# Block 2 of a two-block kernel: own buffers for the meta chunk's matrix, decay gates between the first projections, inverses' copies and second solve in a given order

## The chip, the cores and the metric

The kernel runs on one core of one Trainium2 chip. The metric is the device time of one launch in microseconds. A core has five engines that take their instructions in order, each from its own queue, and that wait for one another with semaphores: TensorE (PE, matrix products), VectorE (DVE), ScalarE (ACT, activations and copies), GpSimd (POOL) and SyncE (SP), which here issues the DMAs. All DMAs of this program that matter below are issued from SP's queue.

## The reference, cut to what matters

Two blocks follow each other. The first (an RWKV-like block) and the mixture of experts at the end are untouched. The change lies in the mixer of the second block: a gated delta rule in two directions, beside a Fourier branch.

```python
proj = hn @ w_in                       # f_in, qkv, z, ab, gate_f, gate_d
f_mix = jnp.real(jnp.fft.fft2(fg, axes=(1, 3), norm="ortho"))
y_f = f_mix.reshape(bsz, seq_len, F_WIDTH) @ w_fourier
qkv = jax.nn.silu(depthwise_conv_centred(qkv, conv_w))
q, k, v = jnp.split(qkv, [QK_WIDTH, 2 * QK_WIDTH], axis=-1)   # then l2-normalised q, k
g_f = -jnp.exp(a_log_f) * jax.nn.softplus(a_f + dt_bias_f)    # decay, and the same backward
beta_f = jax.nn.sigmoid(b_f)
...
# gated_delta_chunked, chunks of 64, 8 heads, both directions
g = jnp.cumsum(g, axis=-1)
decay = jnp.where(lower, jnp.exp(g[..., :, None] - g[..., None, :]), 0.0)
a_mat = jnp.where(strict, (k_beta @ k.T) * decay, 0.0)
t_mat = triangular_solve(eye + a_mat, eye)      # inverse of a 64x64 triangle per chunk and head
u = t_mat @ (v * beta); w = t_mat @ (k_beta * exp(g))
# scan over chunks: v_new = u - w S;  o = q S + qk v_new;  S = S dec + k^T v_new
...
merged = sigmoid(gate_f) * y_f + sigmoid(gate_d) * y_d
return merged @ w_out
```

Sixteen meta tokens stand ahead of the 1024 tokens; they make a short chunk of their own (the "meta chunk"), with a 16 x 16 matrix per head.

## The kernel before, in words

Tokens stand along the free axis in block 2's projections (1040 columns: 16 meta, 1024 tokens), split into pieces of 346 to 348 or, where only the 1024 tokens count, 512 columns. Every fp32 product is made of three matmuls with split operands (`mm3`, L188): a high part `wh`, made by a copy on ACT (L170), and a low part `wl`, made by a subtraction on POOL (L171). Raw weights `wr` come by DMA (L182). The same split makes `fh` and `fl` of the Fourier branch, and `th`, `tl` of its tables `tr`.

A tile framework places the instructions: every engine's queue is filled in an order that follows the code's order and the framework's own estimates, and semaphores are put in where one instruction needs another, or where a buffer of a pool is used again. A pool with one buffer for a name makes the next user wait until every reader of the last one is done.

**Gates.** At the start of the mixer `abT` (L907) holds 32 rows of gate projections. They are transposed (L911, L913, into `m`), become the decay `g` through some twenty small DVE operations (up to `sp`, L944), are summed by a matmul per direction (L947), and the sums go to memory (`GR`, L959).

**Heads loop (from L1107).** For h = 0 to 8 a software pipeline runs the projections of head h (`channels`, L965: k, then q, then v; each a projection, a copy `pr` by ACT L974, and a five-tap convolution: ACT L978, then four DVE steps L980, then silu L981) among the work for head h-1: `decays_in` (L987: loads `gb0`, `gb1`, one per direction, 128 x 9 x 128, broadcast from `GR`, one buffer each), `token_rows` (L999 on: transposes of q and k in `m`, ACT row sums L1000 and L1010, copies `kv` L1002 and L1013, the scales `sk` L1019), `value_rows`, `gram_meta` (the meta chunk's matrix, in a tile `dm0` of which 16 x 16 is used: L1053, exp on ACT L1055, product L1056, stored to `NM` L1058) and `gram` for two halves of the chunks (`dm` L1067, exp L1069, `at` L1083, `qt` L1085; SP stores them as `N`, `QKs` and, of `at`, `OFF`, L1089 to L1094). `dm0` of `gram_meta` and `dm0` of `gram` are two buffers in turn under one name.

**Inverses.** After the heads the 16 x 16 matrices (`xm`) and then two tiles `X` of 64 x 64 matrices, 128 of them each (chunk and head on the partitions), are inverted on DVE, one elimination step after the other: `solve_upper` (L433, L435) for direction 0, `solve_lower` (L417, L419) for direction 1, two operations a step and 62 steps each. `unit` then clears the other triangle by an affine select on POOL (L424) and sets the diagonal (L426). `X` is stored to `TS2` (L1174), its transpose by four ACT copies (L1177) to `TN2` (L1178). One tile `X` and one `t` serve both directions, so the second load of `X` (L1171) waits for all of that.

**Fourier branch.** Beside the inverses TensorE makes the Fourier mix, splits its result into `fh` and `fl`, and runs a loop of 8 x 2 gates (L1240 to L1249): 24 matmuls of `wg` (gate_f), a sigmoid on ACT (L1244), 12 matmuls with `fh`, `fl`, a product on DVE (L1248) and a store (`GF`). PSUM has four buffers `q`. Then come the z and gate_d projections (L1145, L1298) and the recurrence over the chunks (from L1317), which reads `TM`, `TS2`, `TN2` and the stores of the heads loop.

Of the kernel before, what the change touches and what calls it, by code (L numbers as in the profile page):

```python
# [107 lines left out]
NX = 48  # L108

# [21 lines left out]
def body(ctx, tc, A):  # L131
# [770 lines left out]
    with ExitStack() as cg:  # L902
# [5 lines left out]
        q = psm.tile([P, 9, 32], F32, name="m")  # L908
        ab = pg.tile([P, 9, 32], F32, name="ab")
        dve.memset(ab[:, 0], 0.0)  # L910
        pe.transpose(q[:16, 0, :], abT[:, 0:16], ident[:32, :32])  # L911
        for i in range(8):
            pe.transpose(q[:, 1 + i, :], abT[:, 16 + i * P:16 + (i + 1) * P], ident[:32, :32])  # L913
        dve.tensor_copy(ab[:, 1:], q[:, 1:])
        dve.tensor_copy(ab[:16, 0], q[:16, 0])
        dtb = pg.tile([P, 2, H], F32, name="dtb")
        nea = pg.tile([P, 2, H], F32, name="nea")
        for d_, (dt_, al_) in enumerate(((A.dt_bias_fwd_2, A.a_log_fwd_2), (A.dt_bias_bwd_2, A.a_log_bwd_2))):
            sp.dma_start(dtb[:, d_, :], dt_.broadcast_to([P, H]))
            sp.dma_start(nea[:, d_, :], al_.broadcast_to([P, H]))  # L920
        act.activation(nea, nea, AF.Exp)
        dve.tensor_scalar(nea, nea, -1.0, None, op0=OP.mult)
        abv = ab.rearrange("p c (d b h) -> p d b c h", d=2, b=2)
        sh = [P, 2, 9, H]
        xs, ex, z, z2, g = [pg.tile(sh, F32, name=f"sp{i}") for i in range(5)]
        for d_ in range(2):
            act.activation(beta[:, d_], abv[:, d_, 1], AF.Sigmoid)
            dve.tensor_tensor(xs[:, d_], abv[:, d_, 0], dtb[:, d_:d_ + 1, :].to_broadcast([P, 9, H]), op=OP.add)

        act.activation(ex, xs, AF.Abs)  # L930
        act.activation(ex, ex, AF.Exp, scale=-1.0)
        dve.tensor_scalar(z, ex, 2.0, None, op0=OP.add)
        dve.reciprocal(z, z)
        dve.tensor_mul(z, z, ex)
        dve.tensor_mul(z2, z, z)
        dve.tensor_scalar(g, z2, 1.0 / 15, None, op0=OP.mult)
        for i in (13, 11, 9, 7, 5, 3):
            dve.scalar_tensor_tensor(g, g, 1.0 / i, z2, op0=OP.add, op1=OP.mult)
        dve.scalar_tensor_tensor(g, g, 1.0, z, op0=OP.add, op1=OP.mult)
        dve.tensor_scalar(xs, xs, 0.0, None, op0=OP.max)  # L940
        dve.scalar_tensor_tensor(g, g, 2.0, xs, op0=OP.mult, op1=OP.add)
        for d_ in range(2):
            dve.tensor_tensor(g[:, d_], g[:, d_], nea[:, d_:d_ + 1, :].to_broadcast([P, 9, H]), op=OP.mult)
        dve.tensor_scalar(g[:, :, 0], g[:, :, 0], con2("m16"), None, op0=OP.mult)  # L944
        for d_ in range(2):
            q = psm.tile([P, 2, 9, H], F32, name="m")
            pe.matmul(q[:, 0], con2("trif" if d_ == 0 else "trib"), g[:, d_], start=True, stop=True)  # L947
            pe.matmul(q[:, 1], con2("ones"), g[:, d_], start=True, stop=True)
            dve.tensor_copy(gc[:, d_], q[:, 0])
            act.activation(dec[:, d_], q[:, 1], AF.Exp)  # L950
            dve.tensor_tensor(ekd[:, d_], q[:, 1], gc[:, d_], op=OP.subtract)
            act.activation(ekd[:, d_], ekd[:, d_], AF.Exp)
            act.activation(eg[:, d_], gc[:, d_], AF.Exp)
            dve.tensor_scalar(neg[:, d_], eg[:, d_], -1.0, None, op0=OP.mult)
            q = psm.tile([72, P], F32, name="m")
            pe.transpose(q, gc[:, d_].rearrange("p c h -> p (c h)"), ident)
            gr = pg.tile([72, P], F32, name="gr", bufs=2)
            dve.tensor_copy(gr, q)
            sp.dma_start(GR[d_], gr)  # L959
# [87 lines left out]
        def gram_meta(h):  # L1047
# [92 lines left out]

    def z_gate(h):
        w = win2.get(3584 + h * P)
        for half, tt in enumerate(HALF):
            t = pz.tile([P, 512], F32, name="z")
            act.activation(t, half2(w, half), AF.Silu)  # L1145
# [970 lines left out]
```

## Time and profile before

| | |
|---|---|
| median of 3 runs | 3117.06 us (3116.41 to 3122.29) |
| the profiled execution | 3117.2 us |
| its span in the profile | 3115.5 us |
| granted TensorE clock, mean | 0.950 |
| TensorE busy | 2797.8 us (90%) |
| DVE busy | 1516.1 us (49%) |
| ACT busy | 1037.2 us (33%) |
| POOL busy | 887.3 us (28%) |

The profile gives for each engine its busy time, and for each instruction its start, its length, how long its engine stood idle before it and what released it. All times are microseconds from the start of the span of one profiled execution. The granted clock is the share of TensorE's full speed that it was given in a stretch. The stretch of this change reaches from about 1200 us (start of the mixer) to about 2060 us (start of the recurrence).

### The profile page before, as it was taken

To read this page: it belongs to the slowest core of one execution; us is meant where nothing else is said; L and a number is where in the kernel's file an instruction comes from. 1 tells how busy PE (TensorE), PEld (TensorE's weight loads), DVE (VectorE), ACT (ScalarE), POOL (GpSimd) and SP (SyncE) were. 2 spreads that over 40 slices of the span, in tenths; PEclk is the share of its full clock that TensorE was granted. 3 is DMA by queue.
4 is the path that set the end of the run, shared out by engine and by line. 5 is a ranking of instruction groups with operands and counts; after the bars stand their busy time and mean duration, and the time that the engine had idled before them with its cause. 6 is when DMAs were issued, how large, how long until landed. Compare 5 with 4: busy or idle time off the path is not lost. (4 is left out here: it accounts for less than half of the span.)

```text
span 3115.5 us, 42978 instructions
## 1 busy us (share of the span) xinstructions
PE 2797.8 (90%) x16109; PEld 2241.1 (72%) x16109; DVE 1516.1 (49%) x2484; ACT 1037.2 (33%) x2049; POOL 887.3 (28%) x705
## 2 busy tenths in 40 slices
PE   7999999999999998789889859999999987878874
PEld 5777777887787876789888747789888763545442
DVE  3344992324412444566668959724564543222316
ACT  4444112222312443565663221234543221111112
POOL 1233233223324442111115922222465300011011
PEclk9999999999999998899999979999999989999996
DMA  4456415444334543455553332399988659999996
GB/s 116 121 147 208 139 43 167 133 141 121 107 111 152 155 144 71 101 148 136 137 141 106 98 132 69 121 267 267 271 243 269 242 218 411 417 404 413 398 362 257
DMA packets 532932, 599.81 MB, mean 193 GB/s; under 512 B 120779, under 2 KB 429183, under 8 KB 512368
## 3 DMA queue, kind: packets, MB, share of 16 engines
q1 hardware_dynamic: 525808, 582.60, 57.8%
q0 software_dynamic: 6912, 14.43, 1.2%
q8 instruction: 128, 2.10, 0.3%
q14 instruction: 84, 0.69, 0.1%
HBM read 473.23 MB, written 134.44 MB: 195 GB/s over the span
## 5 line engine op out<-in xcount | busy, mean ns | idle before, releaser
L171 POOL TENSOR_TENSOR wl<-wr,wh 128x1024 fp32r<-128x1024 f32 x142 | 353.0, 2486 | 733.9 <-ACT wh L170 724.7
L192 PE MATMUL q<-hTh,wl 128*128 128x512 f32 x1040 | 413.1, 397 | 6.8 <-POOL wl L171 6.8
L191 PE MATMUL q<-hTh,wh 128*128 128x512 f32 x1040 | 416.6, 401 | 2.4 <-DVE t L814 1.4
L193 PE MATMUL q<-hTl,wh 128*128 128x512 f32 x1040 | 417.2, 401 | 0.0
L191 PE MATMUL q<-h2h,wh 128*128 128x346 f32 (+4 forms) x1080 | 389.7, 361 | 4.2 <-ACT wh L170 1.6
L192 PE MATMUL q<-h2h,wl 128*128 128x346 f32 (+4 forms) x1080 | 388.1, 359 | 5.6 <-POOL wl L171 5.6
L193 PE MATMUL q<-h2l,wh 128*128 128x346 f32 (+4 forms) x1080 | 385.6, 357 | 0.0
L192 PEld LDWEIGHTS q<-hTh,wl 128*128 128x128 f32 x1040 | 196.9, 189 | 56.6 <-POOL wl L171 8.3
L191 PEld LDWEIGHTS q<-hTh,wh 128*128 128x128 f32 x1040 | 197.0, 189 | 50.3 <-issue 5.8
L193 PEld LDWEIGHTS q<-hTl,wh 128*128 128x128 f32 x1040 | 197.1, 190 | 46.5 <-issue 3.9
L192 PEld LDWEIGHTS q<-h2h,wl 128*128 128x128 f32 (+1 forms) x1080 | 208.8, 193 | 25.5 <-POOL wl L171 7.1
L191 PEld LDWEIGHTS q<-h2h,wh 128*128 128x128 f32 (+1 forms) x1080 | 208.1, 193 | 25.4 <-ACT wh L170 2.1
L193 PEld LDWEIGHTS q<-h2l,wh 128*128 128x128 f32 (+1 forms) x1080 | 208.8, 193 | 18.6 <-issue 0.2
L170 ACT ACTIVATE wh<-wr 128x1024 fp32r<-128x1024 f32 x142 | 148.4, 1046 | 37.5 <-PE q L193 23.1
L433 DVE TENSOR_TENSOR t<-X 128x62 f32<-128x62 f32 (+30 forms) x124 | 150.0, 1210 | 11.8 <-DMA br<-in_w_branch_dram 7.8
L435 DVE TENSOR_TENSOR X<-X,t 128x62 f32<-128x62 f32 (+30 forms) x124 | 148.9, 1201 | 3.5
L1762 POOL DMA_INDIRECT xg<-HN,gidx x28 | 28.7, 1024 | 375.0 <-PE t L1775 303.9
L1781 PE MATMUL q<-mh,xT 128*64 128x256 f32 (+2 forms) x416 | 102.8, 405 | 20.4 <-DMA mh<-in_w_gate_e_dram 20.2
L1781 PE MATMUL q<-yl,xT 128*32 128x256 f32 (+2 forms) x416 | 103.3, 406 | 19.8 <-DMA yl<-in_w_gate_e_dram 19.3
L1783 ACT ACTIVATE sg<-q 128x256 f32<-128x256 f32 x28 | 10.7, 383 | 326.5 <-PE q L1781 326.5
L1784 DVE TENSOR_TENSOR sg<-sg,q 128x256 f32<-128x256 f32 x28 | 11.8, 421 | 204.7 <-ACT sg L1783 204.7
L591 DVE TENSOR_TENSOR t<-t,q 128x512 f32<-128x512 f32 x32 | 21.9, 686 | 172.7 <-PE q L193 164.6
(624 smaller groups left out, 5979.7 us busy)
## 6 DMA issues: line engine op xcount, KB each, us to landing
wr<-in_w_in_dram SPq DMA_DIRECT2D x125, 512.0 KB, 4.5
d<-in_w_down_e_dram SPq DMA_DIRECT2D x38, 1024.0 KB, 18.9
g<-in_w_gate_e_dram SPq DMA_DIRECT2D x25, 1024.0 KB, 9.5
u<-in_w_up_e_dram SPq DMA_DIRECT2D x25, 1024.0 KB, 13.6
KQ<-KQs SPq DMA_DIRECT2D x32, 512.0 KB, 6.8
KV<-KVs SPq DMA_DIRECT2D x32, 512.0 KB, 6.3
wr<-in_w_gate_e_dram SPq DMA_DIRECT2D x26, 512.0 KB, 17.9
mh<-in_w_gate_e_dram SPq DMA_DIRECT2D x13, 1024.0 KB, 12.9
```

What stands on the lines that cost most here:

```text
L170: act.activation(hi, src, AF.Copy)
L171: pool_e.tensor_sub(lo, src, hi.bitcast(F32))
L191: pe.matmul(out, sh(k), mh(k), start=(k == 0), stop=False)
L192: pe.matmul(out, sl(k), mh(k), start=False, stop=False)
L193: pe.matmul(out, sh(k), ml(k), start=False, stop=(k == kt - 1))
L433: dve.tensor_tensor(t, X[:, 0:s, s:s + 1].to_broadcast([X.shape[0], s, m]), X[:, s:s + 1, s + 1:n].to_broadcast([X.shape[0], s, m]), op=OP ...
L435: dve.tensor_add(X[:, 0:s, s + 1:n], X[:, 0:s, s + 1:n], t)
L591: dve.tensor_mul(sgm, sgm, q)
L1762: nc.gpsimd.indirect_dma_start(out=xg, out_offset=None, in_=HN, in_offset=bass.IndirectOffsetOnAxis(ap=gi, axis=0), bounds_check=S - 1, oo ...
L1781: up[0] = pe.matmul(qs[r_, j], xT[:, k, r_], w[j][k], start=(k == 0), stop=(k == 7))
L1783: si[0] = act.activation(sg, qs[:, 0], AF.Silu)
L1784: dve.tensor_mul(sg, sg, qs[:, 1])
```

## The change

Four things change, all in block 2:

- `gram_meta` takes a tile `dmm` of 16 x 16 with four buffers, in place of `dm0`.
- The code of the gates becomes two functions. `gates_a` (transposes to decay) is called after the first projection of head 0, `gates_b` (sums, exponentials, `GR`) after the second.
- For the two big inverses the affine select is gone, only the diagonal is set (`ones`); the meta matrices keep `unit`. `t` has two buffers.
- `inverse_out(0)`, which stores `X` and its transposes, and the load of the second `X` are placed, on SP and ACT, behind the store and the sigmoid of gate 5 (INV0) of the Fourier loop. The second solve is written as a generator, and five of its steps are handed out after the product of each later gate. `inverse_out(1)` is placed behind the silu of z_gate 6.

```diff
+INV0 = 5
@@ solve_lower
             dve.tensor_add(X[:, s + 1:n, 0:s], X[:, s + 1:n, 0:s], t)
+            yield
@@ start of the mixer: the same lines, now in two functions
+        def gates_a():
...
+        def gates_b():
...
@@ gram_meta
-            dm = pg.tile([P, 4, P], F32, name="dm0", bufs=2)
-            dve.scalar_tensor_tensor(dm[:16, 0, :16], gb[:16, 0, :16], gc[:16, 0, 0, h:h + 1],
+            dm = pg.tile([16, 16], F32, name="dmm", bufs=4)
+            dve.scalar_tensor_tensor(dm, gb[:16, 0, :16], gc[:16, 0, 0, h:h + 1],
                                      con2("dmf")[:16, :16], op0=OP.subtract, op1=OP.min)
...
@@ heads loop
                 channels(h, 0, 8 + h)
                 table_piece(h) if h < 7 else None
+            if h == 0:
+                gates_a()
...
                 channels(h, 1, h)
+            if h == 0:
+                gates_b()
@@ inverses
-    for d_ in range(2):
-        X = pi.tile([P, 64, 64], F32, name="X")
-        t = pi.tile([P, 1024], F32, name="t")
-        sp.dma_start(X, N2[d_])
-        (solve_upper if d_ == 0 else solve_lower)(X, 64, t)
-        unit(X, 64, d_ == 0)
+    def ones(X):
+        return dve.memset(X.rearrange("p i j -> p (i j)")[:, 0:64 * 64:65], 1.0)
+
+    def inverse_out(d_, X):
         sp.dma_start(TS2[d_], X)
         for i in range(4):
-            t = pi.tile([P, 16, 64], F32, name="t")
+            t = pi.tile([P, 16, 64], F32, name="t", bufs=2)
             act.activation(t, X[:, :, 16 * i:16 * i + 16].rearrange("p s t -> p t s"), AF.Copy)
             sp.dma_start(TN2[d_, :, 16 * i:16 * i + 16, :], t)
+    X0, t0 = inverse_in(0)
+    solve_upper(X0, 64, t0)
+    ones(X0)
@@ Fourier loop, after the store of GF
+                n = 2 * d + half
+                if n == INV0:
+                    with tc.issue_after(sent.ins), tc.issue_after(gate.ins):
+                        inverse_out(0, X0)
+                        X1_, t1_ = inverse_in(1)
+                    solve = solve_lower(X1_, 64, t1_)
+                if n > INV0:
+                    with tc.issue_after(mul.ins):
+                        for _ in range(5):
+                            next(solve, None)
+    for _ in solve:
+        pass
+    ones(X1_)
     for h in range(5, H):
         z_gate(h)
+        if h == 6:
+            with tc.issue_after(gated[0].ins):
+                inverse_out(1, X1_)
+            cpi.close()
```

**In the heads loop, SP's queue of the kernel before**, around the two loads for the same later head (`gb_10815` and `gb_10817` are its directions 0 and 1; `at_10551`, `at_10552` and `at_10687` are two halves of the head ahead; `dm_10534` is the meta matrix of that head):

```order
L1094 DMA OFF<-at_10217 64x4x64
L987 DMA gb_10817<-GR 128x9x128
L182 DMA wr<-in_w_in_dram 128x8x128
L1003 DMA KV_8888<-kv 16x128
...
L1092 DMA N_8879<-at_10552 64x4x64
L1094 DMA OFF<-at_10552 64x4x64
L987 DMA gb_10815<-GR 128x9x128
L1058 DMA NM<-dm_10534 16x16
L182 DMA wr<-in_w_in_dram 128x8x128
L1016 DMA KQs<-KQ 128x8x128
L1091 DMA N_8879<-at_10687 64x4x64
```

and of the changed kernel:

```order
L1101 DMA OFF<-at_10081 64x4x64
L184 DMA wr<-in_w_in_dram 128x8x128
L1065 DMA NM<-dmm 16x16
L1024 DMA KQs<-KQ 128x8x128
...
L1101 DMA OFF<-at_10217 64x4x64
L995 DMA gb_10815<-GR 128x9x128
L995 DMA gb_10817<-GR 128x9x128
L184 DMA wr<-in_w_in_dram 128x8x128
L1011 DMA KV_8888<-kv 16x128
```

The load of direction 0 has moved back behind the second half of the head (`at_10217`), directly ahead of that of direction 1, and the store of `NM` no longer follows it.

**DVE's queue at the same place, before** (`dm_11005` is the meta matrix of the head that reads `gb_10815`):

```order
L980 SCALAR_TENSOR_TENSOR KQ<-pr,cw_8899,KQ 128x1040
L1067 SCALAR_TENSOR_TENSOR dm_10675<-gb_10344,gc,C_8877 128x128 x4
L1067 SCALAR_TENSOR_TENSOR dm_11016<-gb_10817,gc,C_8877 128x128 x4
L980 SCALAR_TENSOR_TENSOR KQ<-pr,cw_8899,KQ 128x1040
L1056 SCALAR_TENSOR_TENSOR dm_10534<-m,nbp,dm_10534 16x16
L980 SCALAR_TENSOR_TENSOR KQ<-pr,cw_8899,KQ 128x1040 x2
L1053 SCALAR_TENSOR_TENSOR dm_11005<-gb_10815,gc,C_8877 16x16
L1083 SCALAR_TENSOR_TENSOR at_10687<-g_10691,nbp,dm_10675 128x128 x2
L1085 TENSOR_TENSOR qt_10689<-g_10691,dm_10675 128x256
```

and in the changed kernel:

```order
L1092 TENSOR_TENSOR qt_10219<-g_10229,dm_10210 128x256
L988 SCALAR_TENSOR_TENSOR v<-pr,cw_8899,v 128x1040
L1074 SCALAR_TENSOR_TENSOR dm_10675<-gb_10344,gc,C_8877 128x128 x4
L1074 SCALAR_TENSOR_TENSOR dm_10681<-gb_10346,gc,C_8877 128x128 x4
L988 SCALAR_TENSOR_TENSOR v<-pr,cw_8899,v 128x1040 x3
L1061 SCALAR_TENSOR_TENSOR dmm<-gb_10815,gc,C_8877 16x16
L988 SCALAR_TENSOR_TENSOR KQ<-pr,cw_8899,KQ 128x1040 x3
L1031 TENSOR_SCALAR rq<-ss 128x9
```

The meta matrix has moved from ahead of the second half's `at` to behind that half and the v convolution, ahead of the next k convolution. In both, three or four convolution steps stand between the last reader of the old `gb` (`dm_10675`) and the first reader of the new one.

**POOL's queue at the end of the first big solve, before:**

```order
L171 TENSOR_TENSOR fl<-t_14204,fh 128x512
L171 TENSOR_TENSOR fl<-t_14208,fh 128x512
L424 AFFINE_SELECT X<-X 128x4096
L171 TENSOR_TENSOR fl<-t_14212,fh 128x512
L171 TENSOR_TENSOR fl<-t_14216,fh 128x512
L171 TENSOR_TENSOR wl<-wr,wh 128x1024
```

and in the changed kernel:

```order
L173 TENSOR_TENSOR fl<-t_14048,fh 128x512
L173 TENSOR_TENSOR fl<-t_14052,fh 128x512
L173 TENSOR_TENSOR fl<-t_14056,fh 128x512
L173 TENSOR_TENSOR fl<-t_14060,fh 128x512
L173 TENSOR_TENSOR fl<-t_14064,fh 128x512
L173 TENSOR_TENSOR wl<-wr,wh 128x1024
```

Nothing stands between the pieces of `fl` any more. **DVE's queue at that place, before** (the product of the first gate is `t_14236`):

```order
L435 TENSOR_TENSOR X<-X,t 128x62
L426 MEMSET X 128x64
L1248 TENSOR_TENSOR t_14236<-t_14236,q 128x512
L1248 TENSOR_TENSOR t_14332<-t_14332,q 128x512
L1248 TENSOR_TENSOR t_14278<-t_14278,q 128x512
L1248 TENSOR_TENSOR t_14374<-t_14374,q 128x512
L417 TENSOR_TENSOR t<-X 128x62
```

and in the changed kernel (`t_14080` is the first gate's):

```order
L1190 MEMSET X 128x64
L438 TENSOR_TENSOR X<-X,t 128x62
L1270 TENSOR_TENSOR t_14080<-t_14080,q 128x512
L1270 TENSOR_TENSOR t_14122<-t_14122,q 128x512
...
L1270 TENSOR_TENSOR t_14384<-t_14384,q 128x512
L1270 TENSOR_TENSOR t_14436<-t_14436,q 128x512
L419 TENSOR_TENSOR t<-X 128x62
L421 TENSOR_TENSOR X<-X,t 128x62
L1270 TENSOR_TENSOR t_14500<-t_14500,q 128x512
```

The products still stand behind the whole first solve; eight of them, before four, now stand ahead of the second solve's first step. On ACT the changed kernel has 13 more loads of activation tables than before, two more for most heads; TensorE's order from the Fourier mix on is the same.

## Rows read from the trace of the kernel before

**Rows 1.** Waits of TensorE, 1200 to 2060 us: total, times, longest.
```profile
PE m L1008 <- ACT kv L1002: 39.6, 8, 9.9
PE q L193 <- POOL fl L171: 35.7, 2, 32.6
PE m L913 <- ACT abT L907: 9.2, 2, 8.8
...
PE m L947 <- DVE sp L944: 6.2, 1, 6.2
...
PE g L1078 <- DVE qt L1085: 5.5, 1, 5.5
```
**Rows 2.** Groups by line, DVE: xcount, busy, mean ns, idle before, its releasers.
```profile
L1053 DVE SCALAR_TENSOR_TENSOR dm<-gb,gc,C 16x16 f32<-16x16 f32 x8 | 1.8, 222 | 83.4 <-DMA NM<-dm 73.3 <-DMA gb<-GR 10.0
```
**Rows 3.** Timeline of SP in a head: start, length, line, what, [idle <-releaser].
```profile
1364.65 0.66 SPq L987 DMA_DIRECT2D gb<-GR  x1
...
1384.64 1.03 SPq L987 DMA_DIRECT2D gb<-GR  x1
```
**Rows 4.** Timeline of DVE in the same head.
```profile
1355.48 0.61 DVE L1083 SCALAR_TENSOR_TENSOR at<-g,nbp,dm 128x128 f32<-128x128 f32 x2
...
1363.58 2.64 DVE L980 SCALAR_TENSOR_TENSOR KQ<-pr,cw,KQ 128x1040 f32<-128x1040 f32 x2
1376.14 0.22 DVE L1053 SCALAR_TENSOR_TENSOR dm<-gb,gc,C 16x16 f32<-16x16 f32 x1 [9.92 <-DMA NM<-dm]
```
**Rows 5.** Timeline of ACT in the same head.
```profile
1342.96 0.25 ACT L1002 ACTIVATE kv<-m 16x128 f32<-16x128 f32 x1
...
1376.12 1.28 ACT L1055 ACT_TABLE_LOAD   x1 [8.78 <-DMA NM<-dm]
1377.41 0.21 ACT L1055 ACTIVATE dm<-dm 16x16 f32<-16x16 f32 x1
1377.53 0.43 ACT L974 ACTIVATE pr<-q 128x346 f32<-128x346 f32 x1
1377.87 1.04 ACT L170 ACTIVATE wh<-wr 128x1024 fp32r<-128x1024 f32 x1
...
1391.11 0.25 ACT L1002 ACTIVATE kv<-m 16x128 f32<-16x128 f32 x1
```
**Rows 6.** One head as a window: length, busy (instructions) by engine, clock, DMA, GB/s.
```profile
1342.20:1390.40 48.20, 43.37 (x260) 42.13 (x260) 29.83 (x63) 31.05 (x76) 7.61 (x9) 0.92 0.55 139
```
**Rows 7.** Timeline of POOL at the end of the first solve.
```profile
1791.21 4.27 POOL L171 TENSOR_TENSOR fl<-t,fh 128x512 fp32r<-128x512 f32 x2
1829.26 4.07 POOL L424 TENSOR_SCALAR_AFFINE_SELECT X<-X 128x4096 f32<-128x4096 f32 x1 [33.78 <-DVE X L435]
```
**Rows 8.** Timeline of TensorE at the same place, and at the recurrence's first matmuls.
```profile
1801.40 0.39 PE L193 MATMUL q<-h2l,wh 128*128 128x512 f32 x1
1801.63 0.39 PE L191 MATMUL q<-h2h,wh 128*128 128x512 f32 x1
1834.62 0.80 PE L193 MATMUL q<-fl,bh 128*128 128x512 f32 x1 [32.60 <-POOL fl L171]
...
2045.82 0.49 PE L1324 MATMUL v<-KV,tm 16*16 16x128 f32 x3
```
**Rows 9.** Timeline of DVE in the solves.
```profile
1794.37 2.07 DVE L433 TENSOR_TENSOR t<-X 128x902 f32<-128x902 f32 x1
1796.47 1.10 DVE L435 TENSOR_TENSOR X<-X,t 128x902 f32<-128x902 f32 x1
...
1828.92 0.27 DVE L435 TENSOR_TENSOR X<-X,t 128x62 f32<-128x62 f32 x1
...
1866.66 0.22 DVE L417 TENSOR_TENSOR t<-X 128x62 f32<-128x62 f32 x1 [7.92 <-DMA X<-N]
...
2005.19 0.28 DVE L419 TENSOR_TENSOR X<-X,t 128x62 f32<-128x62 f32 x1
```
**Rows 10.** Timeline of SP: the first load of the recurrence.
```profile
2031.02 0.73 SPq L1317 DMA_DIRECT2D tm<-TM  x1
```

More of the change, by code (lines that the diff above doesn't have):

```diff
@@ L907, in body @@
             act.activation(abT[:, c0:c0 + n], q_ab.pop() if q_ab else proj2(w_ab, c0, n, 32), AF.Copy)
[L908 to L923, printed above, removed]
@@ L935, in body @@
[L935 to L959, printed above, removed]
+        def gates_a():
+            q = psm.tile([P, 9, 32], F32, name="m")
+            ab = pg.tile([P, 9, 32], F32, name="ab")
+            dve.memset(ab[:, 0], 0.0)
+            pe.transpose(q[:16, 0, :], abT[:, 0:16], ident[:32, :32])
+            for i in range(8):
+                pe.transpose(q[:, 1 + i, :], abT[:, 16 + i * P:16 + (i + 1) * P], ident[:32, :32])
+            dve.tensor_copy(ab[:, 1:], q[:, 1:])
+            dve.tensor_copy(ab[:16, 0], q[:16, 0])
+            dtb = pg.tile([P, 2, H], F32, name="dtb")
+            nea = pg.tile([P, 2, H], F32, name="nea")
+            for d_, (dt_, al_) in enumerate(((A.dt_bias_fwd_2, A.a_log_fwd_2), (A.dt_bias_bwd_2, A.a_log_bwd_2))):
+                sp.dma_start(dtb[:, d_, :], dt_.broadcast_to([P, H]))
+                sp.dma_start(nea[:, d_, :], al_.broadcast_to([P, H]))
+            act.activation(nea, nea, AF.Exp)
+            dve.tensor_scalar(nea, nea, -1.0, None, op0=OP.mult)
+            abv = ab.rearrange("p c (d b h) -> p d b c h", d=2, b=2)
+            for d_ in range(2):
+                act.activation(beta[:, d_], abv[:, d_, 1], AF.Sigmoid)
+                dve.tensor_tensor(xs[:, d_], abv[:, d_, 0], dtb[:, d_:d_ + 1, :].to_broadcast([P, 9, H]), op=OP.add)
+            act.activation(ex, xs, AF.Abs)
+            act.activation(ex, ex, AF.Exp, scale=-1.0)
+            dve.tensor_scalar(z, ex, 2.0, None, op0=OP.add)
+            dve.reciprocal(z, z)
+            dve.tensor_mul(z, z, ex)
+            dve.tensor_mul(z2, z, z)
+            dve.tensor_scalar(g, z2, 1.0 / 15, None, op0=OP.mult)
+            for i in (13, 11, 9, 7, 5, 3):
+                dve.scalar_tensor_tensor(g, g, 1.0 / i, z2, op0=OP.add, op1=OP.mult)
+            dve.scalar_tensor_tensor(g, g, 1.0, z, op0=OP.add, op1=OP.mult)
+            dve.tensor_scalar(xs, xs, 0.0, None, op0=OP.max)
+            dve.scalar_tensor_tensor(g, g, 2.0, xs, op0=OP.mult, op1=OP.add)
+            for d_ in range(2):
+                dve.tensor_tensor(g[:, d_], g[:, d_], nea[:, d_:d_ + 1, :].to_broadcast([P, 9, H]), op=OP.mult)
+            dve.tensor_scalar(g[:, :, 0], g[:, :, 0], con2("m16"), None, op0=OP.mult)
@@ new lines, in gates_b @@
+        def gates_b():
+            for d_ in range(2):
+                q = psm.tile([P, 2, 9, H], F32, name="m")
+                pe.matmul(q[:, 0], con2("trif" if d_ == 0 else "trib"), g[:, d_], start=True, stop=True)
+                pe.matmul(q[:, 1], con2("ones"), g[:, d_], start=True, stop=True)
+                dve.tensor_copy(gc[:, d_], q[:, 0])
+                act.activation(dec[:, d_], q[:, 1], AF.Exp)
+                dve.tensor_tensor(ekd[:, d_], q[:, 1], gc[:, d_], op=OP.subtract)
+                act.activation(ekd[:, d_], ekd[:, d_], AF.Exp)
+                act.activation(eg[:, d_], gc[:, d_], AF.Exp)
+                dve.tensor_scalar(neg[:, d_], eg[:, d_], -1.0, None, op0=OP.mult)
+                q = psm.tile([72, P], F32, name="m")
+                pe.transpose(q, gc[:, d_].rearrange("p c h -> p (c h)"), ident)
+                gr = pg.tile([72, P], F32, name="gr", bufs=2)
+                dve.tensor_copy(gr, q)
+                sp.dma_start(GR[d_], gr)
@@ L1144, in z_gate @@
             t = pz.tile([P, 512], F32, name="z")
-            act.activation(t, half2(w, half), AF.Silu)
+            gated[0] = act.activation(t, half2(w, half), AF.Silu)
             sp.dma_start(Z2[h * P:(h + 1) * P, tt], t)
@@ L1167, in body, with inverse_in @@
     sp.dma_start(TM, xm)
-    for d_ in range(2):
+    def inverse_in(d_):
         X = pi.tile([P, 64, 64], F32, name="X")
-        t = pi.tile([P, 1024], F32, name="t")
         sp.dma_start(X, N2[d_])
-        (solve_upper if d_ == 0 else solve_lower)(X, 64, t)
-        unit(X, 64, d_ == 0)
+        return X, pi.tile([P, 1024], F32, name="t", bufs=2)
+    def ones(X):
+        return dve.memset(X.rearrange("p i j -> p (i j)")[:, 0:64 * 64:65], 1.0)
+    def inverse_out(d_, X):
         sp.dma_start(TS2[d_], X)
         for i in range(4):
-            t = pi.tile([P, 16, 64], F32, name="t")
+            t = pi.tile([P, 16, 64], F32, name="t", bufs=2)
             act.activation(t, X[:, :, 16 * i:16 * i + 16].rearrange("p s t -> p t s"), AF.Copy)
             sp.dma_start(TN2[d_, :, 16 * i:16 * i + 16, :], t)
+    X0, t0 = inverse_in(0)
+    solve_upper(X0, 64, t0)
+    ones(X0)
     for g in range(4):
@@ L1243, in body @@
                 sgm = btmp("t2")
-                act.activation(sgm, half2(wg, half), AF.Sigmoid)
+                gate = act.activation(sgm, half2(wg, half), AF.Sigmoid)
                 q = ps.tile([P, 512], F32, name="q")
```

25 lines of the change are left out of this document (9 added, 16 removed).

## The prediction

> **What bounds the kernel now.** I read TensorE's waits first, over the stretch that the change touches. TensorE is busy nearly throughout the kernel, so the change can pay only where TensorE stands still. It does so in four places [rows 1]: 39.6 us over eight heads, for the ACT copy `kv`; 35.7 for `fl`, of which 32.6 at one time; 9.2 and 6.2 for the gates; 5.5 for `qt` at the last head. I then followed each back, engine by engine, to what ended last.
>
> The heads: `kv` stands on ACT behind the exp of the meta matrix, and that behind DVE's L1053, which stood idle 73.3 us over seven heads, by the profile for the store to `NM` [rows 2]. But two loads had to land. `gb` was issued at 1364.65 and L1053 started at 1376.14, 11.5 us later [rows 3, 4], and L1053 reads that `gb`. The store of 16 x 16 is issued right behind it on the same queue. I read the wait as that of `gb`, with the store at most equal.
>
> The inverse: POOL stands 33.78 us at the affine select for the end of the first solve, and the rest of `fl` stands behind it in POOL's queue; TensorE goes on at 1834.62, 5.4 us after the solve's end at 1829.2 [rows 7 to 9].
>
> **The heads, step by step.** The loop of before closes through the single `gb` buffer. Its pieces: `gb` issue to L1053 11.5 (1364.65 to 1376.14); L1053 to the next `kv` 15.0 (1376.14 to 1391.11), as second half, v convolution and v silu stand between; `kv` to the next `gb` issue 21.7 (1342.96 to 1364.65) [rows 3 to 5]. Sum 48.2, the length of the head [rows 6]. So the loop, not TensorE, sets the pace.
>
> After the change `gb` still has one buffer, and its load still stands between the last reader of the old one and the meta matrix, with a few convolution steps under it. Pieces: load 11.5, unchanged. Meta matrix to `kv`: 0.2 for L1053's successor, then on ACT exp 0.2, `pr` 0.4, `wh` 1.0 and a short row sum [rows 4, 5], 2.4 in all. `kv` to the first half's `at`: 1342.96 to 1355.48, 12.5 [rows 4, 5]. First half, convolutions and `dm` up to the second half: 1355.48 to the end of the q convolution at 1363.58 + 2.64, so 10.7 [rows 4]. Second half to `gb` issue: 1376.14 to 1384.64, 8.5 [rows 3, 4]. The two more table loads a head cost 1.28 each [rows 5]; the one ahead of the exp now stands under the wait for `gb`, since it no longer waits for `NM` itself, the other I put on the path: 1.3. Sum 11.5 + 2.4 + 12.5 + 10.7 + 8.5 + 1.3 = 46.9. That is 1.3 to 1.6 less than 48.2 to 48.5; with some of the half-clock time that follows each idle I take 1.7 a head, 11 us over six and a half heads. Bounds: below, -10 (both table loads on the path and another 2 us in the chain, all heads); above, 72 (rival one).
>
> The row after a table load shows the exp 1.29 us after the load's start, so nothing beyond 1.28 [rows 5]. The Trainium skill (ScalarE: Activation LUTs, What ACT_TABLE_LOAD costs) speaks against this change: it gives each switch of sets a further drain of some 1.38 us, 2.66 in all. By that the 13 added loads would be 35 us of ACT time instead of 17, two of them a head would lengthen the loop by up to 2.8, and the heads would give nothing, an estimate from that page; the trace does not show the drain between load and exp.
>
> The last head has no next `gb` to wait for: its second half starts when its own chain is through. The 5.5 us for `qt` [rows 1] go, and some of the half-clock time behind it; I take 8, from 4 to 12.
>
> **The gates.** Nothing is removed, two blocks move. Before, TensorE waits 8.8 for `abT` with nothing to do, then 6.2 for the decay [rows 1]. After, the k projection of head 0 fills about 8 us ahead of the transposes, but both pieces of `abT` must be there before the first transpose, and on ACT they stand behind copies of the tables `tr`, which wait for their loads; so the first wait stays about as long and the second is covered by the q projection. Behind it the two first `gb` loads still come one after the other, ahead of the first k convolution's end. I take 6.2 less 3 for the later `abT`: a gain of 3, between -3 and 8.
>
> **The inverses.** Without the affine select `fl` is no longer held. TensorE then runs into the next wait in the same place: PSUM has four `q`, and the first gate's product stands on DVE behind the whole first solve. So TensorE still waits for the solve's end, but 28 matmuls of 512 columns further on, at 0.23 each 6.5 us of work [rows 8], and goes on 0.7 us after it and not 5.4. That is 11 us.
>
> Against it: POOL now splits three `fl` and one `wl` while DVE is still in the solve. A DVE operation of one size takes 2.07 with POOL busy and 1.10 without [rows 9], and a POOL split of `fl` 2.1 [rows 7]. Some 9.6 us of POOL work then cost the solve half of that, 4.8. The Trainium skill (GPSIMD Engine Reference, Key points) says that GpSimd shares its SBUF interfaces with VectorE and contends with its instructions of two SBUF inputs; the solve's are such, and the rows agree. Net 6 us, and of some 6 us of small waits later in the loop I count 4: 10 in all for TensorE's way to the recurrence.
>
> The second thing to arrive there is the second inverse. Let S be the end of the first solve. Before, the second solve started at S + 37.5 and took 138.8 [rows 9]; the first load of the recurrence was issued 25.5 after its end [rows 9, 10], and its matmuls came at S + 216 [rows 8]. After, the copies and the load of the second `X` stand behind gate 5: 2.5 gates of 36 matmuls, 21 us, the store, four copies, the load: about S + 45, an estimate. Solve: S + 184. No select, two buffers for the copies: 25.5 becomes about 15; the loads follow on SP behind those stores. With 8 us for the loads the recurrence can start at S + 207. TensorE is there at about S + 206, so the two are level. With S 4.8 later, that is again some 5 to 10 us early; I keep 10, from 0 to 18.
>
> **Sum.** 11 + 8 + 3 + 10 = 32. The profiled execution took 3117.2, with 1.7 of that outside its span, and lies within 0.2 of the median. 3117.2 - 32 = 3085.
>
> **Rivals.** One: the store to `NM` was the last to land and `gb` lands early, so no wait is left in the loop and TensorE becomes the bound. Then 39.6 + 5.5 of idle go, and the half clock of a head (0.92 of 48.2, 3.9 us, seven times) [rows 1, 6]: 72. With gates and inverses 3117 - 72 - 13 = 3032. Against it stands that `gb` is issued ahead of `NM`, while it is many times as large (128 x 9 x 128 against 16 x 16); 1 in 10.
>
> Two: the second inverse is last at the recurrence and the table loads eat the loop. Heads give 8 (the last one), gates 0, inverses 0 to 6, since SP's queue holds the recurrence's loads behind the stores of the second inverse: 3105. For it: TensorE and the inverse were level in the sum above; 12 in 100.
>
> Three, slower: both loads of a head now stand back to back on SP. If the 16 DMA engines work on both at once, `gb` of direction 0 lands with direction 1, 11.5 later than it does now. That is 11.5 - 1.7 more a head, 64 over six and a half heads; less 8 + 3 + 10 it gives 3160. It decides from a landing 5 us later (32 / 6.5). Against it: today's load is followed at once by others on the same queue and needs 11.5. Half of this delay would give about 3123; I take 3140 for the case, at 12 in 100.
>
> Four: the change does nothing that counts, since each removed wait was level with another one: 3117, 6 in 100.
>
> **How the numbers follow.** My forecast, 3085, has 60 in 100, with its own range 3066 to 3104 from the bounds of its four terms. Rival one 10, two 12, three 12, four 6. The range 3050 to 3113 takes in the forecast's whole case and rival two, and leaves out rivals one, three and four with the last few points of the forecast. Since about 0.2% (6 us) is what a measurement can tell from no change here, faster holds below 3111: 58 of the forecast's 60, rival one, most of two, 78 in all; slower holds rival three, 12; same the rest, 10.
>
> **What would show it.** In the profile after: L1061 should still wait for `gb` some 6 to 8 us a head, and heads should follow each other every 46 to 48 us; if they do so every 40, rival one was right, and if every 52 or more, rival three, with `gb` landing 16 or more after its issue. POOL should have no idle time at the solve's end; TensorE should wait there about 20 us for the DVE product and not for `fl`. The first solve should be longer than before by about 5. At the recurrence TensorE should wait for nothing over 5 us; if it waits for `TT` or `TN` loads, rival two was right. The forecast is wrong if the chain through the single `gb` isn't what closes the heads' loop.

## The result, and the profile after

The changed kernel takes 3073.19 us (median of 4 runs, 3069.74 to 3077.85) against 3118.8 for the kernel before on the same chips. The ratio is 0.9862, with a 95% interval of 0.9846 to 0.9878: 43 us less, where 32 were forecast. The profiled execution's span went from 3115.5 to 3068.0. A trace is of one execution, and the traces are compared with that in mind: the changed kernel's took 3069.7, the fastest of its four, and that of e6_steps below 3046.8, 7 us above its median.

TensorE's waits in the stretch of the change, 1200 to 2060 us, answer to [rows 1] (total, times, longest):

```profile
PE q L193 <- DVE t L1270: 30.6, 1, 30.6
PE m L1016 <- ACT kv L1010: 18.5, 7, 3.8
PE v L1363 <- DMA KV<-KV: 9.1, 1, 9.1
PE m L921 <- ACT abT L910: 9.0, 2, 6.4
...
PE m L1016 <- ACT kv L1021: 4.7, 1, 4.7
PE q L195 <- POOL fl L173: 4.4, 4, 3.1
```

The wait for `kv` fell from 39.6 to 18.5, with 4.7 more for another copy of that name. The 32.6 us for `fl` at the end of the first solve are gone (4.4 in small pieces are left of 35.7), and 30.6 us for the product of the first gate stand in their place. The one for the decay (6.2) and the one for `qt` (5.5) are gone, and there is a new one of 9.1 us for `KV`, at the start of the recurrence.

**The heads.** First and last `kv` on ACT, of before and of after (timeline: start, length, line, what):

```profile
1293.70 0.25 ACT L1002 ACTIVATE kv<-m 16x128 f32<-16x128 f32 x1
...
1623.63 0.25 ACT L1002 ACTIVATE kv<-m 16x128 f32<-16x128 f32 x1
```

```profile
1282.31 0.25 ACT L1010 ACTIVATE kv<-m 16x128 f32<-16x128 f32 x1
...
1590.65 0.25 ACT L1010 ACTIVATE kv<-m 16x128 f32<-16x128 f32 x1
```

The first comes 11.4 us earlier. From the first to the last of the eight it took 329.9 us and now takes 308.3. By the eight starts of `kv`, the seven turns between them took 49.3, 48.2, 48.5, 48.3, 49.5, 47.9 and 38.3 us before, and take 51.6, 45.2, 45.6, 45.2, 46.8, 46.4 and 27.6 now: 2.3 lost in the first, 13.1 won in the next five, 10.7 in the last. What the meta matrix waits for, in the group that answers to [rows 2], and the landing of the `gb` loads:

```profile
L1061 DVE SCALAR_TENSOR_TENSOR dmm<-gb,gc,C 16x16 f32<-16x16 f32 x8 | 1.8, 223 | 56.5 <-DMA gb<-GR 56.5
```

```profile
DMA to landing us min/median/max: 8.9/12.7/16.5
```

So DVE still stands 7 us a head in front of the meta matrix, and all of it is put down to `gb`. (The trace has the landing of four of the sixteen loads, two pairs.) One turn of the loop, in the same engines as [rows 3 to 5]: SP, DVE, ACT.

```profile
1411.98 1.24 SPq L995 DMA_DIRECT2D gb<-GR  x2
...
1457.57 1.32 SPq L995 DMA_DIRECT2D gb<-GR  x2
```

```profile
1422.75 0.22 DVE L1061 SCALAR_TENSOR_TENSOR dmm<-gb,gc,C 16x16 f32<-16x16 f32 x1 [7.58 <-DMA gb<-GR]
...
1437.91 0.61 DVE L1090 SCALAR_TENSOR_TENSOR at<-g,nbp,dm 128x128 f32<-128x128 f32 x2
...
1450.00 0.61 DVE L1090 SCALAR_TENSOR_TENSOR at<-g,nbp,dm 128x128 f32<-128x128 f32 x2 [1.34 <-PE g L1085]
```

```profile
1416.30 1.28 ACT L1063 ACT_TABLE_LOAD   x1
1423.00 0.21 ACT L1063 ACTIVATE dmm<-dmm 16x16 f32<-16x16 f32 x1 [5.42 <-DVE dmm L1061]
...
1424.66 0.25 ACT L1010 ACTIVATE kv<-m 16x128 f32<-16x128 f32 x1
...
1442.46 1.28 ACT L1076 ACT_TABLE_LOAD   x1
1443.76 0.63 ACT L1076 ACTIVATE dm<-dm 128x512 f32<-128x512 f32 x1
```

The table load for the exp now runs at 1416.30, while the meta matrix still waits; before it came after the wait, at 1376.12 [rows 5].

**The inverses.** POOL, DVE and TensorE at the first solve and behind it, in answer to [rows 7 to 9]:

```profile
1765.01 2.10 POOL L173 TENSOR_TENSOR fl<-t,fh 128x512 fp32r<-128x512 f32 x1 [1.17 <-ACT fh L172]
1767.08 3.25 POOL L173 TENSOR_TENSOR wl<-wr,wh 128x1024 fp32r<-128x1024 f32 x1
1770.28 2.15 POOL L173 TENSOR_TENSOR bl<-br,bh 128x512 fp32r<-128x512 f32 x1
1814.27 2.40 POOL L173 TENSOR_TENSOR wl<-wr,wh 128x1024 fp32r<-128x1024 f32 x1 [41.84 <-ACT wh L172]
```

```profile
1627.33 0.22 DVE L436 TENSOR_TENSOR t<-X 128x62 f32<-128x62 f32 x1
...
1768.11 3.17 DVE L438 TENSOR_TENSOR X<-X,t 128x902 f32<-128x902 f32 x1
1771.32 2.05 DVE L436 TENSOR_TENSOR t<-X 128x882 f32<-128x882 f32 x1
1773.40 1.08 DVE L438 TENSOR_TENSOR X<-X,t 128x882 f32<-128x882 f32 x1
...
1803.58 0.27 DVE L438 TENSOR_TENSOR X<-X,t 128x62 f32<-128x62 f32 x1
...
1856.54 0.22 DVE L419 TENSOR_TENSOR t<-X 128x62 f32<-128x62 f32 x1 [7.20 <-DMA X<-N]
...
1992.85 0.28 DVE L421 TENSOR_TENSOR X<-X,t 128x62 f32<-128x62 f32 x1
```

```profile
1773.51 0.39 PE L195 MATMUL q<-fl,bh 128*128 128x512 f32 x1
1804.50 0.79 PE L193 MATMUL q<-h2h,wh 128*128 128x512 f32 x1 [30.60 <-DVE t L1270]
...
2013.06 1.22 PE L1363 MATMUL v<-KV,tm 16*16 16x128 f32 x5 [9.15 <-DMA KV<-KV]
```

POOL's last piece of `fl` is done by 1767, 37 us ahead of the solve's end; it then waits for nothing of the solve, but for the next weights (41.84). TensorE goes on 0.7 us behind the solve, as the forecast had it. The first solve took 176.5 us (1627.33 to 1803.85).

**Late in the recurrence** something changed that no edit names. The last part of it as windows, before and after (length, then busy (instructions) of TensorE, its weight loads, DVE, ACT, POOL, the granted clock, DMA share, GB/s):

```profile
2254.00:2301.00 47.00, 40.60 (x290) 37.04 (x291) 23.70 (x71) 24.39 (x67) 22.96 (x22) 0.85 0.95 274
```

```profile
2223.00:2254.00 31.00, 29.71 (x249) 27.15 (x248) 21.56 (x60) 17.19 (x51) 19.06 (x20) 1.00 1.03 285
```

Before, TensorE stands still for 6.4 of 47 us there and has a clock of 0.85; after, for 1.3 of 31 at full clock. Windows over the whole stretch from the first state product (`pk`) to the last have these sums, before and after:

```profile
sum 247.00, PE 235.71 PEld 214.45 DVE 109.59 ACT 117.55 POOL 82.35; mean PE 47.14 PEld 42.89 DVE 21.92 ACT 23.51 POOL 16.47
```

```profile
sum 231.00, PE 228.05 PEld 207.90 DVE 110.13 ACT 114.41 POOL 79.99; mean PE 45.61 PEld 41.58 DVE 22.03 ACT 22.88 POOL 16.00
```

TensorE stands idle there for 11.3 us before and for 2.9 after: 8.3 of the 16.7 us in the table below. It works at half clock (1.2 of 2.4 GHz), each time behind such standing idle, for 15.9 us before and for 4.5 after, which is some 6 more. The rest, under 3, is at least in part no gain: 24 short matmuls of this stretch (it has 1911 before, 1887 after) now stand outside it.

The 47.5 us of the two spans, cut at events of both traces:

| stretch | before | after | saved |
|---|---|---|---|
| start to first `kv` | 1293.7 | 1282.3 | 11.4 |
| first to last `kv` | 329.9 | 308.3 | 21.6 |
| last `kv` to start of the first solve | 35.5 | 36.7 | -1.2 |
| first solve | 170.0 | 176.5 | -6.5 |
| its end to the first matmul of the recurrence | 216.1 | 209.2 | 6.9 |
| that to the first state product (`pk`) | 8.9 | 10.4 | -1.5 |
| first to last `pk` | 247.2 | 230.5 | 16.7 |
| from there to the end | 814.1 | 814.0 | 0.1 |

### The profile page after: what moved, and what is told of

Same layout as the page of the kernel before. It is cut to its first block, busy times and chain, and to the rows that moved or that the text cites. A ratio compares the mean times of both kernels' runs of the same rounds, so it can differ in the third digit from the quotient of the medians.

```text
span 3068.0 us, 42973 instructions
## 1 busy us (share of the span) xinstructions
PE 2789.3 (91%) x16109; PEld 2231.9 (73%) x16109; DVE 1517.6 (49%) x2484; ACT 1053.9 (34%) x2062; POOL 880.5 (29%) x703
## 5 line engine op out<-in xcount | busy, mean ns | idle before, releaser
L193 PE MATMUL q<-h2h,wh 128*128 128x346 f32 (+4 forms) x1080 | 387.3, 359 | 33.0 <-DVE t L1270 30.6
L172 ACT ACTIVATE wh<-wr 128x1024 fp32r<-128x1024 f32 x142 | 148.5, 1046 | 38.7 <-PE q L195 24.6
L1822 ACT ACTIVATE sg<-q 128x256 f32<-128x256 f32 x28 | 10.7, 383 | 323.5 <-PE q L1820 323.5
L1820 PE MATMUL q<-yl,xT 128*32 128x256 f32 (+2 forms) x416 | 102.6, 404 | 14.8 <-DMA yl<-in_w_gate_e_dram 14.3
```

The costliest lines, as they stand in the source:

```text
L172: act.activation(hi, src, AF.Copy)
L193: pe.matmul(out, sh(k), mh(k), start=(k == 0), stop=False)
L1820: up[0] = pe.matmul(qs[r_, j], xT[:, k, r_], w[j][k], start=(k == 0), stop=(k == 7))
```

## The experiments

**The three parts, one at a time.** From the kernel before, with one part of the change each:

```diff
@@ e1_dmm, gram_meta alone
-            dm = pg.tile([P, 4, P], F32, name="dm0", bufs=2)
+            dm = pg.tile([16, 16], F32, name="dmm", bufs=4)
@@ e2_gates, the gates alone
+            if h == 0:
+                gates_a()
...
+            if h == 0:
+                gates_b()
@@ e3_inv, the inverses alone (ones, two t, INV0, issue_after, steps)
```

> Only the own buffers for the meta matrix; gates and inverses as before. Theory (the heads' loop closes through the single gb buffer, and the meta matrix's new place shortens it by about 3 us a head): heads follow each other every 45 to 46 us and not 48.3, L1053's successor waits about 7 us a head for gb and for nothing else, and the time falls by about 20 to 25 us, to 3094 to 3099. Rival (the store to NM alone closed the loop): heads every 40 us, 3050. Rival (the gain of the heads in the changed kernel needs the gates' new place): within 6 us of before.

Measured: 3093.72 us, ratio 0.9921 (0.9898 to 0.9943), so 24 to 25 us. That is the theory's number. DVE's wait before the meta matrix is 61.6 us, all of it for `gb`. The first `kv` comes at 1301.9, 8.2 later than before. The turns between the heads then take 43.2 in the mean, with a short last one of 27.6; the six before it take 45.0 to 46.9, as the theory said. The late first head shows in one long wait, the 17.5 in this row of TensorE's waits in the heads:

```profile
PE m L1008 <- ACT kv L1002: 34.6, 7, 17.5
```

> Only the gates' new place. In the trace of the changed kernel the first kv of the heads loop comes 11.4 us earlier than before, where the prediction gave the gates 3. Theory (the gates' place makes this): first kv 8 to 12 us earlier, time 3107 to 3111. Rival (the meta matrix's new buffer and place make it, since the first head also waited for gb): first kv within 3 us of before, time 3115 to 3120.

Measured: 3112.66 us, ratio 0.9982 (0.9972 to 0.9992), 5.6 us; first `kv` at 1287.8, 5.9 earlier. Between the two expectations: the gates' place is worth about six, twice my term, and not the 11.4 of the whole change. The rest of the 11.4 comes only together: the meta matrix alone makes the first head later by 8.2, with the gates moved it makes it earlier by another 5.5.

> Only the inverses: no affine select, copies and second solve in the new order. In the changed kernel's trace TensorE waits 30.6 us for the first gate's product in place of 32.6 for fl, and 9.1 us for KV at the start of the recurrence; yet from there to the end it gains 11 us, late in the recurrence. Theory A (that late gain comes from this part, by the order of loads that it changes): 3100 to 3108. Rival B (the late gain is chance or comes with the earlier start of the whole stage): 3112 to 3119, with the waits late in the recurrence as before.

Measured: 3104.66 us, ratio 0.9954 (0.994 to 0.9968), 14 us. Theory A: the gain late in the recurrence is there (first to last `pk` 231.9 us), and so is the wait for `KV` (8.8 us). The three parts add up to 24.6 + 5.6 + 14.3 = 44.5 by their ratios, against 43 for the whole.

**What closes the heads' loop.** The meta matrices take their decays from a small tile, loaded once:

```diff
+        gm = pg.tile([16, H, 16], F32, name="gm")
...
+                if d_ == 0:
+                    sp.dma_start(gm, GR[0].rearrange("(o c h) t -> o h c t", o=1, h=H)[:, :, 0, 0:16].broadcast_to([16, H, 16]))
...
-            dve.scalar_tensor_tensor(dm, gb[:16, 0, :16], gc[:16, 0, 0, h:h + 1],
+            dve.scalar_tensor_tensor(dm, gm[:, h], gc[:16, 0, 0, h:h + 1],
```

> The changed kernel, but the meta matrices read their decays from a small tile of their own (16 x 8 x 16, loaded once behind the store of GR), not from gb. Theory (what still closes the heads' loop is the load of the single gb, through the meta matrix that waits for it): the wait of 56 us on L1061 is gone, gb has 10 us more until L1074 needs it, TensorE's 18.5 us of waiting for kv go and the half clock behind them; heads every 40 to 42 us, time 3035 to 3050. Rival (another chain through ACT or through the stores of OFF closes the loop at about the same length): heads every 44 to 46 us, 3062 to 3073. Rival (no gain, since L1074 then waits for gb as long): 3070 to 3076.

Measured: 3052.94 us, ratio 0.979 (0.9769 to 0.981), some 20 us under the changed kernel, and from the first to the last `kv` a head takes 40.6 us (284.5 over seven turns). Groups by line on DVE:

```profile
L1077 DVE SCALAR_TENSOR_TENSOR dm<-gb,gc,C 128x128 f32<-128x128 f32 x128 | 35.0, 345 | 16.4 <-DMA gb<-GR 16.4
...
L1064 DVE SCALAR_TENSOR_TENSOR dmm<-gm,gc,C 16x16 f32<-16x16 f32 x8 | 1.7, 228 | 17.4 <-DMA NM<-dmm 13.7 <-DMA gm<-GR 3.6
```

The 56.5 us at the meta matrix became 17.4, and of these none is for `gb`: the meta matrices of four heads now stand ahead of the first head (from 1264.03), and the next four wait for a store to free one of the four buffers. `gb` itself is waited for 16.4 in two places, both in the first head; from the second on nothing waits for it. This is the theory's case, 3 us above the time expected: the load of the one `gb`, through the meta matrix, took part in closing the loop. But the edit did not change the source alone. The framework placed ACT's queue anew too, and it has 100 loads of activation tables in place of 112, two fewer a head. The five middle turns went from 45.8 to 41.1 in the mean; of these 4.8 us up to 2.6 can be the two loads of 1.28. No run separates the two.

**What closes the stage of the inverses.**

```diff
@@ e5_inv2, from e4_gm
-INV0 = 5
+INV0 = 2
```

> The kernel of the run e4_gm with INV0 = 2: the first inverse's stores and the second load of X stand behind gate 2, not gate 5. Theory (the way from the end of the heads to the recurrence is closed by the chain first solve, stores, load, second solve, stores, with 53 us between the two solves in the changed kernel): the second solve starts 20 to 28 us earlier, TensorE's 9.2 us of waiting for KV at the recurrence go, the 28 us for the first gate's product stay; time 9 to 12 us under e4_gm, 3041 to 3045. Rival (ACT's copies, now ahead of the sigmoids of gates 3 to 5, hold TensorE as they did before): TensorE waits another 5 us or more in the Fourier loop, time as e4_gm or above.

Measured: 3054.45 us, ratio 0.9788 (0.9771 to 0.9805): level with e4_gm, and so 9 to 13 us off the theory, though its mechanism came as told. The second solve started 29 us behind the first one's end, not 53, the wait for `KV` is gone, and from the last `kv` to the first matmul of the recurrence it took 413.0 us, where e4_gm took 422.7. But waits late in the recurrence were back, as before the change, and from the first to the last `pk` it took 243.9 in place of 237.0 (TensorE, 1640 to 2300 us; the first row is the stall at the first gate, which stays):

```profile
PE q L193 <- DVE t L1273: 28.4, 1, 28.4
...
PE v L1416 <- DVE zt L1476: 3.6, 1, 3.6
PE q L1444 <- ACT W L1439: 3.3, 1, 3.3
```

The rival's time came, but not its reason: there is no new wait in the Fourier loop.

```diff
@@ e6_steps, from e4_gm
-    solve_upper(X0, 64, t0)
-    ones(X0)
+    first = upper_steps(X0, 64, t0)
+    for _ in range(40):
+        next(first)
...
+                if n < 4:
+                    with tc.issue_after(mul.ins):
+                        for _ in range(6):
+                            next(first, None)
+                if n == 3:
+                    ones(X0)
```

with INV0 = 4; `upper_steps` is `solve_upper` as a generator.

> The kernel of e4_gm with the last 22 steps of the first solve too handed out among the products of gates 0 to 3, stores and second load behind gate 4. Theory (the chain of solves closes the stage): TensorE's 28 us for the first gate's product are gone, but as the second solve ends no more than 10 us earlier, TensorE waits 25 to 40 us at the recurrence's start for its loads, and the time falls by no more than 5 to 12 us, 3041 to 3048. Rival (the wait for the product is worth its 28 us and 8 of half clock by itself): 3017 to 3025.

Measured: 3039.55 us, ratio 0.9743 (0.9726 to 0.9759): 13 us under e4_gm, the fastest kernel here. The 28.4 us are gone, TensorE's wait for `KV` is 14.4:

```profile
1970.25 1.86 PE L1382 MATMUL v<-KV,tm 16*16 16x128 f32 x8 [14.44 <-DMA KV<-KV]
```

The theory's time holds nearly (3041 to 3048 were expected), its 25 to 40 us at the recurrence do not. The first matmul of the recurrence came 18 us earlier than in e4_gm for 28.4 us of stall removed. Another 5 were lost in the heads of this execution: e4_gm and the four kernels built on it have the same queues up to the last `kv`, and reach it at 1565.8 (e4_gm) to 1573.4, here at 1570.7. The last 5 are back in front of the second inverse's loads, 14.4 against 9.2. So the chain of the two solves does close the stage from behind, but 10 us later than I thought. Then the recurrence gave back more: from the first to the last `pk` 250.5 us against 237.0, with queues that changed once more (table below).

**Where the late gain comes from.**

```diff
@@ e7_out, from e3_inv
+    inverse_out(1, X1_)
+    cpi.close()
     for h in range(5, H):
         z_gate(h)
-        if h == 6:
-            with tc.issue_after(gated[0].ins):
-                inverse_out(1, X1_)
-            cpi.close()
```

> The kernel of e3_inv, but the stores of the second inverse are written right behind its solve, as before, and not behind z_gate 6. Question: where the 11 us come from that kernels with the inverses' part gain late in the recurrence. Theory (this placement changes the order of loads in the recurrence's queues): the late gain shrinks to under 4 us and the 9 us for KV at the start go or change. Rival (it comes with the other edits of this part): the late gain stays at 9 to 12 us.

Measured: 3105.58 us in a single run; first to last `pk` 232.8 us, the late gain stays, and so does the wait at the start:

```profile
PE v L1353 <- DMA KV<-KV: 9.0, 1, 9.0
```

But this run tests nothing. The framework made the same program of the other place in the code: by operation and tile, all five engines of e7_out have the same instructions in the same order as those of e3_inv. The last store of the second inverse and the first load of the recurrence on SP, in e3_inv and in e7_out:

```profile
2035.70 0.32 SPq L1189 DMA_DIRECT2D TN<-t  x1
...
2036.60 0.90 SPq L1348 DMA_DIRECT2D tm<-TM  x1
```

```profile
2040.09 0.32 SPq L1189 DMA_DIRECT2D TN<-t  x1
...
2040.99 1.07 SPq L1346 DMA_DIRECT2D tm<-TM  x1
```

So it is a second measurement of e3_inv (231.9 and 232.8), and the place of these stores was not tested by it. That their place in the code is not enough, e5_inv2 shows: it has them behind z_gate 6 too, and no late gain. I then laid the queues of all kernels side by side from the first `pk` on:

| kernel | queues in the recurrence as in | wait for `KV` | first to last `pk` |
|---|---|---|---|
| before | before | none | 247.2 |
| e1_dmm | before | none | 244.1 |
| e2_gates | before | none | 245.9 |
| e5_inv2 | before | none | 243.9 |
| changed | changed | 9.1 | 230.5 |
| e3_inv | changed | 8.8 | 231.9 |
| e4_gm | changed | 9.2 | 237.0 |
| e7_out | changed | 9.0 | 232.8 |
| e6_steps | neither | 14.4 | 250.5 |

The order of the recurrence, which the framework sets by its own estimates, comes in two kinds, and length and wait go with the kind. In the first kind eight groups of three matmuls of gate_d stand behind the first matmuls of the meta chunk; here in the kernel before:

```profile
2045.26 1.04 PE L1324 MATMUL v<-KV,tm 16*16 16x128 f32 x8
2046.23 0.51 PE L191 MATMUL q<-h2h,wh 128*128 128x512 f32 x1
```

In the second, and in e6_steps, they stand ahead of the whole recurrence (in the changed kernel the last one starts at 2003.52, and the wait of 9.15 for `KV` follows), and nothing covers the loads of `KV`. Between the first and the last `pk` there are equally many matmuls of gate_d in both kinds, 144. I first took it that they stand between the chunks in the second kind, and that led to a theory on these fillers, for the last two runs:

```diff
@@ e8_fill8 from e5_inv2, e9_fill7 from e6_steps
-NFILL = 9
+NFILL = 8
...
-NFILL = 9
+NFILL = 7
```

> The kernel of e5_inv2 with NFILL = 8 in place of 9: one unit of gate_d less ahead of the recurrence, one more to fill in between its chunks. In the runs so far the stretch from the first to the last state product of the recurrence took 244 to 247 us where the queues stand there as in the kernel before, with no wait at its start, and 231 to 237 where they stand as in the changed kernel, with 9 us of waiting for KV at its start; e4_gm and e5_inv2 came out level in sum. Theory (what decides is whether filler matmuls are left between the late chunks): the stretch takes 232 to 240 us, and as the second inverse is early here the start waits under 5 us; time 3042 to 3049. Rival (the late waits are made by the load on the DMA queues, and a wait at the start only moves them): the stretch stays above 243 or the start waits 9 us, time within 5 us of e5_inv2, 3050 to 3058.

> The kernel of e6_steps with NFILL = 7 in place of 9. TensorE is 14 us too early at the recurrence there, and its stretch took 250 us. Theory (fillers between the late chunks decide): stretch 235 to 242 us, the wait at the start 14 to 25 us, since less work lies ahead of it; time 3028 to 3038. Rival (the DMA load decides the end of the recurrence): the end of the recurrence comes no earlier, time 3036 to 3045.

Measured: e8_fill8 3054.34 us (ratio 0.9793, 0.9768 to 0.9818), level with e5_inv2; first to last `pk` 248.7. e9_fill7 3051.13 us (0.9773, 0.9755 to 0.979), 12 us over e6_steps; 254.0, with this wait at the start:

```profile
PE v L1382 <- DMA KV<-KV: 24.7, 1, 24.7
```

Both stretches hold more matmuls than before (one and two units of gate_d, each 24 of 0.23 us, 5.5 us), and even without these they stay at 243. So fillers held back for the chunks do not bring the late gain; the theory falls. e8_fill8 meets the rival's numbers, e9_fill7 neither its nor the theory's. What the gain is made of is told above: less idle time of TensorE and less half clock. Why the changed order of the queues leaves fewer waits, 7 to 17 us by the kernels compared, stays open; two traces of the same queues, of the changed kernel and e4_gm, already differ by 6.5. The DMA engines are busy nearly all of that time in both (shares 0.95 and 1.03 in the windows above), but no run shows that they set it.

## Why the prediction was right, and where it was wrong

**The size.** The sign and the range held; the sum was 11 us short. By parts alone, and by stretches of the changed kernel's trace:

| term | forecast | part alone | stretch in the changed kernel |
|---|---|---|---|
| gates | 3 | 5.6 | 11.4, to the first `kv` (with the first head) |
| heads' loop | 11 | 24.6, both terms | 10.8, first six turns |
| last head | 8 | | 10.7, last turn |
| inverses | 10 | 14.3 | -2.3 to the first `pk`, 16.7 from there |

**The heads' loop** was the right mechanism, with each piece near its size. Forecast and measured, from the rows above: load 11.5 and 10.8 (1411.98 to 1422.75), meta matrix to `kv` 2.4 and 1.9, `kv` to the first half 13.8 with its table load and 13.25, first to second half 10.7 and 12.1, second half to the next issue 8.5 and 7.6. Sum 46.9 and 45.6, against 48.2 before. These pieces are cut at events of one turn, before as after, so that they add up to its length whatever sets the pace; "so the loop, not TensorE, sets the pace" did not follow from the sum. What speaks for the loop is the wait of 56.5 us and e4_gm. A turn won 2.6 where 1.7 stood in the sum; over the six turns the first one's loss took that back, so that 11 and 10.8 agree partly by luck. The last head won 10.7, inside its bounds of 4 to 12.

**The table loads** cost 1.28 each and nothing more: ACT's busy time rose by 16.7 us (1037.2 to 1053.9), 13 loads of 1.283. The drain that the Trainium skill adds (ScalarE: Activation LUTs, What ACT_TABLE_LOAD costs) does not show in the trace after either: the exp of `dm` starts at 1443.76, 1.30 after its load's start at 1442.46. The part alone gained 24.6, not nothing, so the row was the one to go by. That the loads cost the loop something is not excluded: e4_gm has 12 fewer.

**The gates** are the term that was mis-sized: 3 in the sum, 5.6 alone, and 11.4 with the first head. In the changed kernel the wait for `abT` stayed at 9.0 as said, and the one for the decay went. What I missed is that gates and meta matrix are one term at the first head: the one alone loses 8.2 to the first `kv`, the other wins 5.9, both win 11.4.

**The inverses** are where a step failed, though their sum came out near. Right: `fl` free, TensorE caught by the first gate's product, going on 0.7 behind the solve, the solve longer by POOL's work. The solve grew by 6.5 where 4.8 were forecast, and the wait was 25.1 in e3_inv and 30.6 in the changed kernel, where "about 20" was said; that the 5.5 more come of the shorter heads is argued, not shown. Wrong: "the two are level" at the recurrence. Its loads on SP stood behind the second inverse's stores, TensorE waited 9.1 us, as rival two had it. With S for the end of the first solve, TensorE was there at S + 200, not S + 206. The loads had landed at S + 209, where S + 207 was said, and within that the estimate of 45 for the start of the second solve was short, at 52.7, while the solve itself and the loads took 5 less than said. And wrong by omission: the order of the recurrence. I compared the queues up to the recurrence's start and took the rest as unchanged; that TensorE's order is the same from the Fourier mix on, as said above, does not hold. 16.7 us of the 47.5 lie in the recurrence.

**The rivals.** One fell: all 56.5 us at the meta matrix are waits for `gb`, and taking `gb` away (e4_gm) gave what rival one had promised for `NM`, in part. Three fell: in the two pairs of loads whose landing the trace has, direction 0 landed 8.9 and 10.4 us after its issue and direction 1 15.0 and 16.5. Two held in its first half alone, for 9 us.

## What to carry to other kernels

A wait for "a or b" is settled by giving the reader another source for one of them: with a tile of 512 bytes a partition `gb` was no longer waited for, and 20 us went, where the buffer that the profile named had taken off 25. Such an edit can move other things in the queues (there two table loads a head), and a move in the code can change nothing in them (e7_out): compare the queues before reading a time. When an edit lets a scheduler place things anew, compare the queues to the end of the program and not to the end of the edited stage; here a third of the gain lay behind it. A stall that an edit takes away is worth only what the rest leaves of it: 28 us of stall gave 13, as 5 came back in the next wait and 13 went, in the trace, in a recurrence whose order had changed.

## What the runs showed of the hardware

When DVE in the solve and POOL in a split both work on SBUF, they seem to take turns, one whole instruction each. In the rows of the inverses above, POOL's `wl` ends at 1770.33, DVE's addition of 128 x 902 at 1771.28, POOL's `bl` at 1772.43, DVE's multiply of 128 x 882 at 1773.37: each ends 0.94 to 1.15 us after the other's last one, about its own length without the other. By themselves the next DVE operations took 1.05 to 1.08,

```profile
1774.51 1.05 DVE L436 TENSOR_TENSOR t<-X 128x860 f32<-128x860 f32 x1
```

and the splits for `bl` 1.30 in the median, while beside the other engine DVE's took 2.05 and 3.17 and the splits for `fl` 1.85 to 2.22. That it is turns is read from these rows, not tested by a run. So work that POOL is spared from waiting is not free: the first solve grew from 170.0 to 176.5 us.

Two broadcast loads of the same size issued back to back on one queue do not share the engines evenly: in the two pairs whose landing is known, the first lands about as one does alone (8.9 and 10.4 us after its issue, before 10.6 to 11.2), the second 15.0 and 16.5 us after its own.
